# A third seven-product tile in the second matrix of a feed-forward layer, with one sum fewer per tile and later side work

## The chip, the cores and the metric

The kernel runs on one core of a Trainium2 chip. The metric is device time in microseconds of one launch. TensorE (PE) multiplies matrices into eight PSUM banks of 128 x 512 f32; VectorE (DVE) and ScalarE (ACT) do the elementwise work; SyncE (SP) issues the loads of weights.

## The reference

The reference is an encoder trunk of two layers over 256 tokens of width 2048. The change touches the feed-forward part of both layers:

```
def sq_relu_mlp(h, w1, w2):
    return jnp.square(jax.nn.relu(h @ w1)) @ w2

for i in range(DEPTH):                       # 2
    ... x = x + attention(rms_norm(x, ...))
    x = x + sq_relu_mlp(rms_norm(x, g), w1, w2)
return rms_norm(x, final_norm)
```

x is (1, 256, 2048) in float32, w1 is 2048 x 8192 and w2 is 8192 x 2048.

## The kernel before

Each float32 matrix is split into a high part that TensorE takes as it is (`wh`, by a cast on ACT) and the rest (`wl`, by a subtract on DVE); a product of two such matrices is three matmuls (`three`, L193).

A feed-forward layer (`ffn`) runs in four groups g. A group makes 2048 of the 8192 inner columns with two calls of `gemm_pair` on w1 (cp 0 and 1, 1024 columns each) and multiplies them by their rows of w2 with two more calls. A call is eight steps, called tiles here and counted from 1; tile n reads one weight block of 128 x 4 x 512 (two k-blocks by two column blocks), and its left matrix is pair k (two k-blocks of 128) of the normalized x, or of the inner activations `hT`. The tokens are two blocks, so a tile is a product of 2 x 2 block matrices.

A plain tile (kind "s") does the eight block products, 24 matmuls, into four banks named "2", "3", "4", "S". A tile of kind "x" does seven products in Strassen's manner (Winograd's form), 21 matmuls, of which some go to four more banks, "1", "5", "6", "7". It takes sums of weight blocks, made by `prep_x`: `sums` on DVE, their high parts `hs` on ACT, their low parts `ls` on DVE. It also takes sums of the left blocks, made once by `sums_and_parts` (four small subtracts on DVE, two casts on ACT, two subtracts on DVE). After the last x tile, `begin` combines banks "1", "6", "7", "5" into the tile `C`. `last_sum` (w1) or `early` and `put` (w2, into x) finish the sums. For w1 the result in `C` passes through relu and square on ACT (`squared_relu`), is transposed on TensorE in four groups of four, r = 0 to 3, each into a bank that the running call hasn't begun to use ("1", "6", "7", "5" in this order), and is read from there into `hT`.

FF_PAIRS = (3, 5) are the x tiles of all calls: tiles 4 and 6 of eight. The last call of a layer (g = 3, cp = 1) has another order of tiles, in which they are tiles 5 and 6 in the first layer and 3 and 5 in the second.

The order is written by hand. In step i, after each quarter's products, the program issues the side work that was attached to that quarter (`after`, `tasks`) and one part of the preparation of step i + 2:

```
        for n in range(4):
            s.quarters(s, n)
            ...
            elif i and n < 3:
                prep(i + 2, n)
        ...
        prep(i + 2, 3)
        load(i + 5)
```

Engines run their own queues in this order and wait for each other by semaphores. `w` has three buffers, `wh` and `wl` four each (two tiles' worth), `sums` one, `hs` and `ls` two.

Of the kernel before, what the change touches and what calls it, by code (L numbers as in the profile page):

```python
# [8 lines left out]
F32 = mybir.dt.float32  # L9
F32R = mybir.dt.float32r  # L10
# [4 lines left out]
P = 128  # L15
# [13 lines left out]
class Step:  # L29
# [6 lines left out]
    def __init__(self, kind, loads, quarters):  # L36
        self.kind = kind
        self.loads = loads
        self.quarters = quarters
        self.evac = []  # L40
        self.after = [[] for _ in range(4)]
        self.tasks = [[] for _ in range(4)]
        self.post = []
        self.hi, self.lo = [None] * 8, [None] * 8


@with_exitstack
def tile_encoder(ctx: ExitStack, tc: tile.TileContext, ins, out):
# [115 lines left out]
    def prep_x(s, n):  # L164

        w = s.w
        if n == 0:
            t = s.sums = part.pool.tile([P, 4, 512], F32, name="sums", tag="sums", bufs=1)
            add(nc.vector, t[:, 0:2, :], w[:, 1:3, :], w[:, 0, :].unsqueeze(1).to_broadcast([P, 2, 512]))
            add(nc.vector, t[:, 2, :], t[:, 1, :], w[:, 1, :])  # L170
            add(nc.vector, t[:, 3, :], t[:, 2, :], w[:, 3, :])
        elif n == 1:
            hi, lo = two_parts(s, 1)
            split(hi, lo, w[:, 2:4, :])
            s.hs = part.pool.tile([P, 4, 512], F32R, name="hs", tag="hs", bufs=2)
            nc.scalar.copy(s.hs, s.sums)  # L176
        elif n == 2:
            ls = part.pool.tile([P, 4, 512], F32R, name="ls", tag="ls", bufs=2)
            subtract(nc.vector, ls, s.sums, s.hs.bitcast(F32))
            for a in range(4):  # L180
                s.hi[4 + a], s.lo[4 + a] = s.hs[:, a, :], ls[:, a, :]
        else:
            hi, lo = two_parts(s, 0)
            split(hi[:, 1, :], lo[:, 1, :], w[:, 1, :])

    def block(w, k, c):
        return w[k, c // 512].rearrange("p (a n) -> p a n", n=512)
# [92 lines left out]
    def gemm_pair(w, cp, A, sums_of, order, finish, split_end=False):  # L280
        made, q = [], {}
        first_x = [n for n, o in enumerate(order) if o[0] == "x"]
        touched = set()

        def left(pair, which):

            t, u = A[pair // 2], 2 * (pair % 2)
            if which in ("S2", "S3", "S4"):
                c = sums_of[pair]
                return [c[:, h, ("S3", "S2", "S4").index(which), :] for h in range(2)]  # L290
            a, ts_ = {"A11": (0, 0), "A12": (1, 0), "S1": (0, 1), "A21": (0, 1), "A22": (1, 1)}[which]
            return [t[:, u + a, h, ts_ * P:(ts_ + 1) * P] for h in range(2)]

        def product(bank, a, b, last):
            if not q:
                q.update({k: banks[:, n, :] for k, n in sum_banks().items()})
            three(q[bank], a, b, bank not in touched, last)
            touched.add(bank)

        X = (("1", "A11", 2), ("2", "A12", 3), ("6", "S2", 6), ("7", "S3", 4), ("4", "A22", 7), ("3", "S4", 1),  # L300
             ("5", "S1", 5))

        for n, (kind, pair) in enumerate(order):
            k, u = pair // 2, pair % 2
            loads = [(w[k, 2 * cp + c].rearrange("p (a n) -> p a n", n=512)[:, 2 * u:2 * u + 2, :],
                      2 - 2 * c, 4 - 2 * c) for c in (1, 0)]
            if kind == "x":
                def quarter(s, m, pair=pair, n=n):
                    for bank, a, b in X[2 * m:2 * m + 2]:
                        product(bank, left(pair, a), (s.hi[b], s.lo[b]), n == first_x[-1] and bank in "1567")  # L310
            else:
                def quarter(s, m, pair=pair, n=n):
                    tb, c = QUARTERS[m]
                    for kk in range(2):
                        b = 2 * (1 - c) + kk
                        a = (("A11", "A12"), ("A21", "A22"))[tb][kk]
                        product(STD[tb, c], left(pair, a), (s.hi[b], s.lo[b]), n == len(order) - 1 and kk == 1)
            s = Step(kind, loads, quarter)
            s.even = pair % 2 == 0
            steps.append(s)  # L320
            made.append(s)

        if split_end:
            ends = made[-2:]
            for e, s in enumerate(ends):
                def quarter(s, m, e=e):
                    tb, m = m // 2, m % 2
                    pair = order[len(order) - 2 + m][1]
                    for kk in range(2):
                        b = 2 * (1 - e) + kk  # L330
                        a = (("A11", "A12"), ("A21", "A22"))[tb][kk]
                        product(STD[tb, e], left(pair, a), (ends[m].hi[b], ends[m].lo[b]), m == 1 and kk == 1)
                s.quarters = quarter

        def begin(m):
            if m == 0:
                C = q["C"] = part.pool.tile([P, 4, 512], F32, name="C", tag="C")
                nc.scalar.copy(C[:, 0, :], q["1"])
                subtract(nc.vector, C[:, 1, :], q["6"], C[:, 0, :])
            elif m == 1:  # L340
                subtract(nc.vector, q["C"][:, 2, :], q["C"][:, 1, :], q["7"])
            elif m == 2:
                add(nc.vector, q["C"][:, 1::2, :], q["C"][:, 1:3, :], q["5"].unsqueeze(1).to_broadcast([P, 2, 512]))

        s = made[first_x[-1] + 1]
        for m in range(3):
            s.after[0 if s is made[-1] else m].append(lambda m=m: begin(m))
        finish(made, q)
        return made
# [305 lines left out]
        return pending_norm(lambda: norms[n], n == 2)  # L655

    FF_PAIRS = (3, 5)
    FF_ORDER = [("x" if k in FF_PAIRS else "s", k) for k in range(8)]

    parts = {len(steps) + 9: "feed-forward"}  # L660
    out_rows(ins["na_wo"], na_oT, 4, lambda: norms[1], begin_norm(1, False, FF_PAIRS),
# [2 lines left out]

    def ffn(norm, w1, w2, next_norm, next_done):
        for g in range(4):
            hT, sums = [None] * 4, {}

            def hidden(made, q, cp, hT=hT, sums=sums):
                i = steps.index(made[-1]) + 1  # L670

                def squared_relu(tb, n):
# [7 lines left out]
                for r in range(4):  # L680
# [10 lines left out]
                    def post(r=r, held=held):  # L691
                        c, half, pair = 2 * cp + r // 2, r % 2, 4 * cp + r
                        if half == 0:
                            hT[c] = opool.tile([P, 4, 2, T], F32R, name="hT", tag="o")
                        if pair in FF_PAIRS:
                            raw = scratch([P, 2, T], "h")
                            nc.scalar.copy(raw, held["t"])
                            sums[pair] = part.pool.tile([P, 2, 3, P], F32R, name="hs", tag="hsum", bufs=len(FF_PAIRS))
                            sums_and_parts(raw, hT[c], half, sums[pair])
                        else:  # L700
                            to = hT[c][:, 2 * half:2 * half + 2]
                            split(to[:, :, 0, :], to[:, :, 1, :], held["t"])

                    at(i + 1 + r // 2, pe, post, quarter=r % 2 * 2)

            for cp in range(2):
                gemm_pair(w1, 2 * g + cp, norm.xT, norm.sums, FF_ORDER, lambda made, q, cp=cp: hidden(made, q, cp))

            w2g = w2[4 * g:4 * (g + 1)]
            last = g == 3  # L710

            def to(cp, tb, c):
                return x[:, tb, cp * 1024 + c * 512:cp * 1024 + (c + 1) * 512]

            def residual(made, q, cp, parted):
                def put(tb, c):
                    add(nc.vector, to(cp, tb, c), to(cp, tb, c), q[STD[tb, c]])

# [7 lines left out]
                        add(nc.vector, to(cp, 1, 1), to(cp, 1, 1), C[:, 3, :])  # L726

                if not parted:
                    for n in range(2):
                        made[-1].after[n].append(lambda n=n: early(n))  # L730
                    for m, (tb, c) in enumerate(QUARTERS):
                        made[-1].after[m].append(lambda tb=tb, c=c: put(tb, c))
                    if last:
                        for c in (2 * cp, 2 * cp + 1):
                            made[-1].post.append(lambda c=c: next_norm().squares(c))
                            if next_done is not None:
                                next_done(made[-1], c, c % 2)
                    return
# [15 lines left out]

            for cp in range(2):
                parted = last and cp == 1
                order = FF_ORDER
                if parted:
                    order = [FF_ORDER[k] for k in ((0, 1, 2, 4, 3, 5, 6, 7), (0, 1, 3, 2, 5, 4, 6, 7))[next_done is None]]
                gemm_pair(w2g, cp, hT, sums, order, lambda made, q, cp=cp, parted=parted: residual(made, q, cp, parted),  # L760
                          parted)

    ffn(norms[1], ins["ffn0_w1"], ins["ffn0_w2"], lambda: norms[2], begin_norm(2, True))
# [361 lines left out]
```

## Time and profile before

| | |
|---|---|
| median of 3 runs | 2296.74 us (2296.55 to 2297.01) |
| profiled execution | 2296.8 us, of it the span 2295.0 us |
| granted TensorE clock, mean | 0.998 |
| PE / PEld / DVE / ACT busy | 99% / 83% / 77% / 53% |
| DVE, all subtracts `wl<-w,wh` | 931.7 us, 802 of them |
| DVE, `ls<-sums,hs` | 146.7 us, 64 of them |
| DVE, waiting for `hs` ahead of `ls` | 44.4 us, 64 times |

The first number of a group in the profile is its busy time, then the mean of one in ns, then the idle time of that engine just before them with what ended it. A wait row reads: the engine and its line, what it waited for, us in total, times, the longest. A timeline row reads: start, duration, engine, line, operation, written from read.

### The profile page before, as it was taken

How to read it: one execution, taken by the hardware profiler on the slowest of the kernel's cores; microseconds unless marked ns; L12 is line 12 of the kernel's file. 1: busy time of each engine (PE TensorE's matmuls, PEld its weight loads, DVE VectorE, ACT ScalarE, POOL GpSimd, SP SyncE). 2: the span in 40 equal slices, each digit the busy share in tenths (PEclk: the TensorE clock that was granted, in tenths of full speed). 3: DMA queues.
4: the chain of work that ended last, by engine and by line, in shares of the span. 5: the costliest groups of instructions: out<-in, count | busy, mean ns of one | idle time of the engine just before them, and what ended most of it. 6: DMA issues, size and time to landing. Idle time of an engine off the chain costs nothing.

```text
span 2295.0 us, 28363 instructions
## 1 busy us (share of the span) xinstructions
PE 2269.6 (99%) x10988; PEld 1898.5 (83%) x10988; DVE 1758.1 (77%) x2065; ACT 1217.3 (53%) x1526; POOL 0.7 (0%) x6
## 2 busy tenths in 40 slices
PE   9999999999999999999999999999999999999998
PEld 7888888888888888888888888888888888888886
DVE  6666766788788788788877667757788788788787
ACT  6454545664565565465444544456654554554554
POOL 0000000000000000000000000000000000000000
PEclk9999999999999999999999999999999999999999
DMA  7566555656656656655555545545566566566563
GB/s 249 170 179 179 184 179 175 192 171 217 199 166 218 198 170 211 198 178 183 184 194 168 185 169 180 179 167 164 183 210 193 184 205 198 183 202 202 183 218 131
DMA packets 110727, 430.33 MB, mean 188 GB/s; under 512 B 23872, under 2 KB 24448, under 8 KB 92160
## 3 DMA queue, kind: packets, MB, share of 16 engines
q1 hardware_dynamic: 109920, 426.82, 57.7%
q8 instruction: 86, 1.41, 0.2%
q10 hardware_dynamic: 672, 1.70, 0.2%
q14 instruction: 49, 0.40, 0.0%
HBM read 426.38 MB, written 2.10 MB: 187 GB/s over the span
## 4 chain that ended last, share of the span: by engine, by line
PE 94%; DVE 3%; ACT 1%; DMA 1%; issue 1%; SPq 0%; ACTq 0%; DVEq 0%
PE banks L196 24%; PE banks L197 24%; PE banks L195 24%; PE banks L220 13%; PE banks L222 7%; PE banks L688 1%; DMA bias<-in_rpb_dram 1%; DVE wl L191 1%; PE banks L378 1%; ACT wh L190 1%; DVE x L136 0%; DVE sums L136 0%; PE banks L880 0%; PE banks L840 0%; PE banks L591 0%
## 5 line engine op out<-in xcount | busy, mean ns | idle before, releaser
L191 DVE TENSOR_TENSOR wl<-w,wh 128x1024 fp32r<-128x1024 f32 (+1 forms) x802 | 931.7, 1176 | 378.4 <-ACT wh L190 373.9
L190 ACT CAST wh<-w 128x1024 fp32r<-128x1024 f32 (+1 forms) x802 | 804.0, 1014 | 685.5 <-PE banks L197 447.7
L220 PE MATMUL banks<-xT,wh 128*128 128x512 f32 x1280 | 454.0, 398 | 0.9 <-ACT wh L190 0.7
L195 PE MATMUL banks<-wh,xT 128*128 128x512 f32 x1152 | 453.9, 394 | 0.0
L196 PE MATMUL banks<-wl,xT 128*128 128x512 f32 x1152 | 448.9, 390 | 0.9 <-DVE wl L191 0.9
L197 PE MATMUL banks<-wh,xT 128*128 128x512 f32 x1152 | 449.6, 390 | 0.0
L222 PE MATMUL banks<-xT,wl 128*128 128x256 f32 x1280 | 358.4, 280 | 2.3 <-DVE wl L191 2.3
L195 PE MATMUL banks<-wh,hT 128*128 128x512 f32 x832 | 327.7, 394 | 0.0
L197 PE MATMUL banks<-wh,hT 128*128 128x512 f32 x832 | 324.7, 390 | 0.0
L196 PE MATMUL banks<-wl,hT 128*128 128x512 f32 x832 | 323.9, 389 | 0.0
L220 PEld LDWEIGHTS banks<-xT,wh 128*128 128x128 f32 x1280 | 240.8, 188 | 55.6 <-ACT wh L190 1.8
L197 PEld LDWEIGHTS banks<-wh,xT 128*128 128x128 f32 x1152 | 216.3, 188 | 45.6
L196 PEld LDWEIGHTS banks<-wl,xT 128*128 128x128 f32 x1152 | 216.6, 188 | 44.8 <-DVE wl L191 1.9
L195 PEld LDWEIGHTS banks<-wh,xT 128*128 128x128 f32 x1152 | 216.5, 188 | 42.9
L222 PEld LDWEIGHTS banks<-xT,wl 128*128 128x128 f32 x1280 | 242.3, 189 | 3.4 <-DVE wl L191 3.2
L176 ACT CAST hs<-sums 128x2048 fp32r<-128x2048 f32 x64 | 122.5, 1914 | 153.2 <-DVE sums L136 153.2
L197 PEld LDWEIGHTS banks<-wh,hT 128*128 128x128 f32 x832 | 156.2, 188 | 33.2
L196 PEld LDWEIGHTS banks<-wl,hT 128*128 128x128 f32 x832 | 156.4, 188 | 31.6
L195 PEld LDWEIGHTS banks<-wh,hT 128*128 128x128 f32 x832 | 156.3, 188 | 31.3
L133 DVE TENSOR_TENSOR ls<-sums,hs 128x2048 fp32r<-128x2048 f32 x64 | 146.7, 2293 | 44.4 <-ACT hs L176 44.4
L136 DVE TENSOR_TENSOR sums<-sums,w 128x512 f32<-128x512 f32 x128 | 88.6, 692 | 4.4
L136 DVE TENSOR_TENSOR sums<-w 128x1024 f32<-128x1024 f32 x64 | 78.0, 1219 | 0.0
(187 smaller groups left out, 2142.0 us busy)
## 6 DMA issues: line engine op xcount, KB each, us to landing
w<-in_ffn_w_dram SPq DMA_DIRECT2D x512, 512.0 KB, 5.0
w<-in_dil_wqkv_dram SPq DMA_DIRECT2D x72, 1024.0 KB, 4.9
w<-in_na_wqkv_dram SPq DMA_DIRECT2D x47, 1024.0 KB, 5.1
w<-in_na_wo_dram SPq DMA_DIRECT2D x16, 1024.0 KB, 4.9
w<-in_dil_wo_dram SPq DMA_DIRECT2D x8, 1024.0 KB, 4.9
bias<-in_rpb_dram SPq DMA_DIRECT2D x32, 96.0 KB, 9.0
out_dram<-x SPq DMA_DIRECT2D x8, 256.0 KB, 2.5
x<-in_x_dram SPq DMA_DIRECT2D x3, 512.0 KB, 9.6
```

The costliest lines, as they stand in the source:

```text
L133: engine.tensor_tensor(out=out, in0=a, in1=b, op=ALU.subtract)
L136: engine.tensor_tensor(out=out, in0=a, in1=b, op=ALU.add)
L176: nc.scalar.copy(s.hs, s.sums)
L190: nc.scalar.copy(dst_hi, src)
L191: nc.vector.tensor_tensor(out=dst_lo, in0=src, in1=dst_hi.bitcast(F32), op=ALU.subtract)
L195: nc.tensor.matmul(o, left[0], right[0], start=start, stop=False)
L196: nc.tensor.matmul(o, left[0], right[1], start=False, stop=False)
L197: nc.tensor.matmul(o, left[1], right[0], start=False, stop=stop)
L220: nc.tensor.matmul(o, s.hi[a][:, cs], xt.rearrange("p h t -> p (h t)"), start=first, stop=False)
L222: nc.tensor.matmul(o[:, :T], s.lo[a][:, cs], xt[:, 0, :], start=False, stop=last)
L378: nc.tensor.transpose(self.tp[:, a, tb * P:(tb + 1) * P], x[:, tb, kt * P:(kt + 1) * P], ident)
L688: nc.tensor.transpose(t[:, a, tb * P:(tb + 1) * P], q["C"][:, 2 * tb + f // 4, f % 4 * P:(f % 4 + 1) * P], ident)
```

## The change

For the second matrix of groups 0 to 2 of both layers, pair 2 joins the x tiles. The order of pairs becomes 0, 1, 2, 4, 3, 6, 5, 7, so that x tiles are tiles 3, 5 and 7. The first matrix and the whole last group keep two.

The sum that A22 takes is added into the weight tile itself (`w[:, 0]`) and split there with `w[:, 1]`; `sums`, `hs` and `ls` are three blocks wide instead of four. This holds for all x tiles of the kernel.

The sums of the inner activations (`parts_of`) are moved from the tile of the transposes to later ones: pair 2 in tile 5, pair 3 in tile 6 of the second call, pair 5 in tile 4 of the third. The transposes of the second call's result, until now two groups in each of tiles 2 and 3 of the third call, are all in tile 2, in groups 0 to 2. `early`, the addition of C to x, moves from the last tile to tiles 3 and 5, or 4 and 6, of the next call. Since the last x tile is now tile 7, the three parts of `begin` all stand in tile 8.

```diff
@@ class Step
-        self.hi, self.lo = [None] * 8, [None] * 8
+        self.hi, self.lo = [None] * 7, [None] * 7
@@ prep_x
-            t = s.sums = part.pool.tile([P, 4, 512], F32, name="sums", tag="sums", bufs=1)
+            t = s.sums = part.pool.tile([P, 3, 512], F32, name="sums", tag="sums", bufs=1)
...
-            add(nc.vector, t[:, 3, :], t[:, 2, :], w[:, 3, :])
+            add(nc.vector, w[:, 0, :], t[:, 2, :], w[:, 3, :])
...
-            s.hs = part.pool.tile([P, 4, 512], F32R, name="hs", tag="hs", bufs=2)
+            s.hs = part.pool.tile([P, 3, 512], F32R, name="hs", tag="hs", bufs=2)
...
-            split(hi[:, 1, :], lo[:, 1, :], w[:, 1, :])
+            split(hi, lo, w[:, 0:2, :])
@@ gemm_pair
-        X = (... ("7", "S3", 4), ("4", "A22", 7), ("3", "S4", 1),
+        X = (... ("7", "S3", 4), ("4", "A22", 0), ("3", "S4", 1),
@@ ffn
+            last = g == 3
+            pairs2 = FF_PAIRS if last else (2, 3, 5)
@@ hidden
-                        if pair in FF_PAIRS:
-                            raw = scratch([P, 2, T], "h")
+                        if pair in pairs2:
+                            raw = part.pool.tile([P, 2, T], F32, name="h", tag="h", bufs=2)
                             nc.scalar.copy(raw, held["t"])
-                            sums[pair] = part.pool.tile([P, 2, 3, P], F32R, name="hs", tag="hsum", bufs=len(FF_PAIRS))
-                            sums_and_parts(raw, hT[c], half, sums[pair])
+
+                            def parts_of(c=c, half=half, raw=raw, pair=pair):
+                                sums[pair] = part.pool.tile([P, 2, 3, P], F32R, name="hs", tag="hsum", bufs=3)
+                                sums_and_parts(raw, hT[c], half, sums[pair])
+                            steps[i + (3 if cp else 2 + r)].after[1].append(parts_of)
...
-                    at(i + 1 + r // 2, pe, post, quarter=r % 2 * 2)
+                    if cp and not last:
+                        at(i + 1, pe, post, quarter=r)
+                    else:
+                        at(i + 1 + r // 2, pe, post, quarter=r % 2 * 2)
@@ residual
                 if not parted:
+                    i = steps.index(made[-1])
                     for n in range(2):
-                        made[-1].after[n].append(lambda n=n: early(n))
+                        if last:
+                            made[-1].after[n].append(lambda n=n: early(n))
+                        else:
+                            at_after(i + 1 + (2 + 2 * n if cp else 3 + 2 * n), 1, lambda n=n: early(n))
@@ second product
-                order = FF_ORDER
+                order = range(8) if last else (0, 1, 2, 4, 3, 6, 5, 7)
...
-                gemm_pair(w2g, cp, hT, sums, order, ...
+                gemm_pair(w2g, cp, hT, sums, ff_order(pairs2, order), ...
```

How it stands in the queues of ACT and DVE, at three places of a group. First ACT's queue at the start of the third call (w2, cp 0), tile 1 and the start of tile 2. The rows from C are relu and square of one quarter each; `hT<-banks` reads a transposed group, and `h<-banks` one whose sums are made. Before:

```order
L190 CAST wh<-w 128x1024 x4
L674 ACTIVATE C<-C,rstd 128x512
L675 ACTIVATE C<-C 128x512
L674 ACTIVATE C<-C,rstd 128x512
L675 ACTIVATE C<-C 128x512
L190 CAST wh<-w 128x1024
L674 ACTIVATE C<-C,rstd 128x512
L675 ACTIVATE C<-C 128x512
L674 ACTIVATE C<-C,rstd 128x512
L675 ACTIVATE C<-C 128x512
L190 CAST wh<-w 128x1024
L190 CAST hT<-banks 128x2x256
```

After (the lines of the file have moved by four):

```order
L190 CAST wh<-w 128x1024 x4
L678 ACTIVATE C<-C,rstd 128x512
L679 ACTIVATE C<-C 128x512
L678 ACTIVATE C<-C,rstd 128x512
L679 ACTIVATE C<-C 128x512
L190 CAST wh<-w 128x1024
L176 CAST hs<-sums 128x1536
L678 ACTIVATE C<-C,rstd 128x512
L679 ACTIVATE C<-C 128x512
L678 ACTIVATE C<-C,rstd 128x512
L679 ACTIVATE C<-C 128x512
L190 CAST wh<-w 128x1024
```

The cast `hs` of the first x tile, which is tile 3 now, has come between the second and the third pair of relu and square.

Second, DVE's queue for the x tile 6 of the second call (w1, cp 1), from the subtract of the tile ahead. Before, the sums of pair 3's activations stand ahead of that tile's `sums`:

```order
L133 TENSOR_TENSOR c<-h 128x128
L133 TENSOR_TENSOR c<-h,c 128x128
L133 TENSOR_TENSOR hT<-h,hT 128x2x256
L133 TENSOR_TENSOR hs<-c,hs 128x384
L191 TENSOR_TENSOR wl<-w,wh 128x1024
L136 TENSOR_TENSOR sums<-w 128x1024
L136 TENSOR_TENSOR sums<-sums,w 128x512 x2
L191 TENSOR_TENSOR wl<-w,wh 128x1024
L133 TENSOR_TENSOR ls<-sums,hs 128x2048
```

After:

```order
L191 TENSOR_TENSOR wl<-w,wh 128x1024 x3
L136 TENSOR_TENSOR sums<-w 128x1024
L136 TENSOR_TENSOR sums<-sums,w 128x512
L136 TENSOR_TENSOR w<-sums,w 128x512
L191 TENSOR_TENSOR wl<-w,wh 128x1024
L133 TENSOR_TENSOR ls<-sums,hs 128x1536
L191 TENSOR_TENSOR wl<-w,wh 128x1024
L133 TENSOR_TENSOR c<-h 128x128
```

The sums of the activations (`c<-h` and on) have gone behind the x tile's preparation, and the last of the weight sums is written into `w`.

Third, DVE's queue at the end of a w2 call, tile 8. Before:

```order
L136 TENSOR_TENSOR C<-C,banks 128x2x512
L191 TENSOR_TENSOR wl<-w,wh 128x1024
L136 TENSOR_TENSOR x<-x,C 128x1024
L136 TENSOR_TENSOR x<-x,banks 128x512
L133 TENSOR_TENSOR x<-x,C 128x512
L136 TENSOR_TENSOR x<-x,C 128x512
L136 TENSOR_TENSOR x<-x,banks 128x512
L191 TENSOR_TENSOR wl<-w,wh 128x1024
L136 TENSOR_TENSOR x<-x,banks 128x512 x2
```

After:

```order
L133 TENSOR_TENSOR C<-banks,C 128x512
L133 TENSOR_TENSOR C<-C,banks 128x512
L136 TENSOR_TENSOR C<-C,banks 128x2x512
L136 TENSOR_TENSOR x<-x,banks 128x512 x2
L191 TENSOR_TENSOR wl<-w,wh 128x1024
L136 TENSOR_TENSOR x<-x,banks 128x512 x2
L191 TENSOR_TENSOR wl<-w,wh 128x1024
```

The three operations on `C` now stand directly ahead of the additions of the banks to x, and the three additions of C to x are no longer there.

More of the change, by code (lines that the diff above doesn't have):

```diff
@@ L174, in prep_x @@
             split(hi, lo, w[:, 2:4, :])
-            s.hs = part.pool.tile([P, 4, 512], F32R, name="hs", tag="hs", bufs=2)
+            s.hs = part.pool.tile([P, 3, 512], F32R, name="hs", tag="hs", bufs=2)
             nc.scalar.copy(s.hs, s.sums)
         elif n == 2:
-            ls = part.pool.tile([P, 4, 512], F32R, name="ls", tag="ls", bufs=2)
+            ls = part.pool.tile([P, 3, 512], F32R, name="ls", tag="ls", bufs=2)
             subtract(nc.vector, ls, s.sums, s.hs.bitcast(F32))
-            for a in range(4):
+            for a in range(3):
                 s.hi[4 + a], s.lo[4 + a] = s.hs[:, a, :], ls[:, a, :]
@@ L298, in product @@
             touched.add(bank)
-        X = (("1", "A11", 2), ("2", "A12", 3), ("6", "S2", 6), ("7", "S3", 4), ("4", "A22", 7), ("3", "S4", 1),
+        X = (("1", "A11", 2), ("2", "A12", 3), ("6", "S2", 6), ("7", "S3", 4), ("4", "A22", 0), ("3", "S4", 1),
              ("5", "S1", 5))
@@ L657, in tile_encoder, with ff_order @@
     FF_PAIRS = (3, 5)
-    FF_ORDER = [("x" if k in FF_PAIRS else "s", k) for k in range(8)]
+    def ff_order(pairs, order=range(8)):
+        return [("x" if k in pairs else "s", k) for k in order]
     parts = {len(steps) + 9: "feed-forward"}
@@ L666, in ffn, with hidden @@
         for g in range(4):
+            last = g == 3
+            pairs2 = FF_PAIRS if last else (2, 3, 5)
             hT, sums = [None] * 4, {}
-            def hidden(made, q, cp, hT=hT, sums=sums):
+            def hidden(made, q, cp, hT=hT, sums=sums, pairs2=pairs2, last=last):
                 i = steps.index(made[-1]) + 1
@@ L702, in post, with residual @@
                             split(to[:, :, 0, :], to[:, :, 1, :], held["t"])
-                    at(i + 1 + r // 2, pe, post, quarter=r % 2 * 2)
+                    if cp and not last:
+                        at(i + 1, pe, post, quarter=r)
+                    else:
+                        at(i + 1 + r // 2, pe, post, quarter=r % 2 * 2)
             for cp in range(2):
-                gemm_pair(w1, 2 * g + cp, norm.xT, norm.sums, FF_ORDER, lambda made, q, cp=cp: hidden(made, q, cp))
+                gemm_pair(w1, 2 * g + cp, norm.xT, norm.sums, ff_order(FF_PAIRS), lambda made, q, cp=cp: hidden(made, q, cp))
             w2g = w2[4 * g:4 * (g + 1)]
-            last = g == 3
             def to(cp, tb, c):
                 return x[:, tb, cp * 1024 + c * 512:cp * 1024 + (c + 1) * 512]
-            def residual(made, q, cp, parted):
+            def residual(made, q, cp, parted, last=last):
                 def put(tb, c):
@@ L756, in ffn @@
                 parted = last and cp == 1
-                order = FF_ORDER
+                order = range(8) if last else (0, 1, 2, 4, 3, 6, 5, 7)
                 if parted:
-                    order = [FF_ORDER[k] for k in ((0, 1, 2, 4, 3, 5, 6, 7), (0, 1, 3, 2, 5, 4, 6, 7))[next_done is None]]
-                gemm_pair(w2g, cp, hT, sums, order, lambda made, q, cp=cp, parted=parted: residual(made, q, cp, parted),
+                    order = ((0, 1, 2, 4, 3, 5, 6, 7), (0, 1, 3, 2, 5, 4, 6, 7))[next_done is None]
+                gemm_pair(w2g, cp, hT, sums, ff_order(pairs2, order), lambda made, q, cp=cp, parted=parted: residual(made, q, cp, parted),
                           parted)
```

## The prediction

> **What bounds the kernel now.** A "tile" is one step of eight in a call of `gemm_pair`; a "plain" tile does eight block products, an "x tile" seven. I read the page first, then the chain of waits, then the stretches tile by tile, then TensorE's own waits.
>
> ```profile
> span 2295.0 us, 28363 instructions
> PE 2269.6 (99%) x10988; PEld 1898.5 (83%) x10988; DVE 1758.1 (77%) x2065; ACT 1217.3 (53%) x1526; POOL 0.7 (0%) x6
> PE 94%; DVE 3%; ACT 1%; DMA 1%; issue 1%; SPq 0%; ACTq 0%; DVEq 0%
> ```
>
> TensorE (PE) is busy all the time and carries 94% of the chain. DVE at 77% is an average; what counts is whether it keeps ahead in the tiles that change. One second-product call with its neighbours, by call (from and to; length; busy time and instructions of PE, PEld, DVE, ACT, POOL; granted clock, DMA share, GB/s):
>
> ```profile
> 580.93:623.27 42.34, 42.34 (x187) 34.92 (x186) 34.41 (x35) 20.09 (x19) 0.00 (x0) 1.00 0.64 197
> 623.27:667.77 44.50, 44.50 (x204) 36.42 (x203) 36.30 (x41) 27.39 (x33) 0.00 (x0) 1.00 0.59 189
> 667.77:712.05 44.28, 44.28 (x204) 36.48 (x203) 36.48 (x41) 27.40 (x33) 0.00 (x0) 1.00 0.59 190
> 712.05:754.39 42.34, 42.34 (x187) 34.92 (x186) 34.59 (x35) 20.10 (x19) 0.00 (x0) 1.00 0.63 198
> ```
>
> These are the four calls of one group: two of the first matrix, two of the second. The third, by tile (tiles 1, 2, 4, 6, 8):
>
> ```profile
> 667.77:673.21 5.44, 5.44 (x26) 4.50 (x25) 2.86 (x4) 5.15 (x8) 0.00 (x0) 1.00 0.64 194
> 673.21:679.58 6.37, 6.37 (x34) 5.29 (x33) 4.03 (x5) 4.32 (x6) 0.00 (x0) 1.00 0.44 134
> 685.95:690.82 4.87, 4.87 (x23) 3.95 (x21) 4.78 (x8) 4.26 (x6) 0.00 (x0) 1.00 0.46 135
> 696.31:701.17 4.86, 4.86 (x23) 3.93 (x22) 4.86 (x5) 3.04 (x4) 0.00 (x0) 1.00 0.35 78
> 706.61:712.05 5.44, 5.44 (x26) 4.50 (x25) 5.01 (x6) 2.11 (x2) 0.00 (x0) 1.00 0.72 239
> ```
>
> A plain tile takes 5.44 us for 24 matmuls (0.227 each), an x tile 4.86 for 21 (0.231 each), at a granted clock of 1.00. Tile 2 with two groups of four transposes takes 0.93 more, so 0.465 a group. The only waits of TensorE inside the feed-forward calls are these:
>
> ```profile
> PEld banks L196 <- DVE ls L133: 5.9, 10, 1.6
> PE banks L196 <- DVE ls L133: 2.1, 2, 1.2
> ```
>
> They are for `ls`, the low parts of the sums of an x tile. One of the eight small ones, then the two large ones (in the last calls, where x tiles stand elsewhere):
>
> ```profile
> 653.12 0.39 PE L195 MATMUL banks<-hs,xs 128*128 128x512 f32 x1
> 653.46 0.50 PE L196 MATMUL banks<-ls,xs 128*128 128x512 f32 x1
> 653.80 0.40 PE L197 MATMUL banks<-hs,xs 128*128 128x512 f32 x1
> ...
> 1088.81 0.39 PE L195 MATMUL banks<-hs 128*128 128x512 f32 x1
> 1090.36 0.51 PE L196 MATMUL banks<-ls,hs 128*128 128x512 f32 x1 [1.16 <-DVE ls L133]
> ...
> 2253.23 0.39 PE L195 MATMUL banks<-hs 128*128 128x512 f32 x1
> 2254.57 0.50 PE L196 MATMUL banks<-ls,hs 128*128 128x512 f32 x1 [0.95 <-DVE ls L133]
> ```
>
> From start to start 0.23 is normal. The first costs 0.68 - 0.46 = 0.22, the others 1.55 - 0.23 = 1.3 and 1.34 - 0.23 = 1.1.
>
> **The change, part by part.**
>
> *Twelve tiles become x tiles* (three groups, two calls, two layers). Each drops 3 matmuls. By the rows that is 5.44 - 4.86 = 0.58; the other end is 3 x 0.227 = 0.68, if a new x tile kept a plain tile's pace. I take 0.58, since all x tiles shown run at it: 12 x 0.58 = **-7.0 us** (end: -8.2). [...]
>
> *The sums shrink from four to three.* What an x tile's preparation costs now:
>
> ```profile
> 646.45 1.22 DVE L136 TENSOR_TENSOR sums<-w 128x1024 f32<-128x1024 f32 x1
> 647.71 1.42 DVE L136 TENSOR_TENSOR sums<-sums,w 128x512 f32<-128x512 f32 x2
> 649.05 1.22 DVE L191 TENSOR_TENSOR wl<-w,wh 128x1024 fp32r<-128x1024 f32 x1
> 651.11 2.29 DVE L133 TENSOR_TENSOR ls<-sums,hs 128x2048 fp32r<-128x2048 f32 x1 [0.84 <-ACT hs L176]
> ...
> L191 DVE TENSOR_TENSOR wl<-w,wh 128x512 fp32r<-128x512 f32 x68 | 46.3, 684 | 0.0
> L190 ACT CAST wh<-w 128x1024 fp32r<-128x1024 f32 x734 | 764.2, 1051 | 685.5 <-PE banks L197 447.7 <-PE banks L220 174.4 <-DVE x L136 23.3
> L176 ACT CAST hs<-sums 128x2048 fp32r<-128x2048 f32 x64 | 122.5, 1914 | 153.2 <-DVE sums L136 153.2
> ```
>
> From first sum to the end of `ls` is 6.95 us, and DVE stands 0.84 of it waiting for `hs`. After, between the 1024 and 2048 wide rows, `hs` of 1536 takes 1.48 and `ls` 1.76 (estimates), and the copy can start 0.7 earlier, since it no longer awaits the last 512-wide sum (1.42 for two). DVE then doesn't stand: 2.6 + 1.2 + 1.76, about 5.5 us, so `ls` is there **1.4 earlier**. Given back is a split of 1024 for 512 (1.22 for 0.68) behind `ls`; its half is first used by A22 in the third quarter, 1.4 us after `ls` is, and is ready 1.1 after it. The DVE work of a preparation stays 6.8 (1.22 + 1.42 + 1.22 + 1.76 + 1.22). So the two large waits (1.3, 1.1) go: **-2.4**. The eight small ones go too: their tile is prepared 1.4 earlier, and the 2.5 us of sums of activations that stood ahead of it moves behind it:
>
> ```profile
> 642.51 0.29 DVE L133 TENSOR_TENSOR c<-h 128x128 f32<-128x128 f32 x1
> ...
> 644.48 0.55 DVE L133 TENSOR_TENSOR hs<-c,hs 128x384 fp32r<-128x384 f32 x1
> ```
>
> (642.51 to 645.03.) That is 8 x 0.22 = **-1.8**. If something else is late there: 0.
>
> *DVE's added work*, costed at nothing, with DVE's own idle time as cover. A plain preparation is 2 x 1.22 = 2.4, an x one 6.8: +4.4 for each second-product call, which makes 36.5 + 4.4 = 40.9 in the third call (its end is then near 43.7) and 34.6 + 4.4 = 39.0 in the fourth (of 41.8), before the additions to x that leave the third for the fourth. In steady alternation DVE has 6.8 + 2.4 = 9.2 for each 5.44 + 4.86 = 10.3 of TensorE; once a group the sums of pair 5 make it 11.7, and 1.4 of backlog are worked off in the next two pairs. Preparation runs up to two tiles ahead, so a lag of that size is covered. In the second call it is 36.3 + 2.5 - 0.7 = 38.1 of 44.3. If the cover is gone, `ls` is late again, at 0.2 to 1.3 a tile, the range of the rows above.
>
> *Four transposes in tile 2 of the third call*, no longer two each in tiles 2 and 3: the same 4 x 0.465 on TensorE, no gain or loss. But the first x tile comes one tile sooner, and its first product writes the bank from which the first transposes are read. What stands before that read on ACT:
>
> ```profile
> 667.97 1.05 ACT L190 CAST wh<-w 128x1024 fp32r<-128x1024 f32 x1 [1.67 <-PE banks L197]
> 668.92 0.72 ACT L674 ACTIVATE C<-C,rstd 128x512 f32<-128x512 f32 x1
> ...
> 670.96 0.63 ACT L675 ACTIVATE C<-C 128x512 f32<-128x512 f32 x1
> 671.49 1.03 ACT L190 CAST wh<-w 128x1024 fp32r<-128x1024 f32 x1
> ```
>
> Counted from the call's start at 667.77: the second cast ends at +4.75; then, newly, `hs` (1.5, to +6.2), two more pairs of relu and square (2.6, to +8.8), a cast (1.0), DVE's subtract behind it (1.2, to +11.0) and the read of the bank (0.7, to +11.7). The x tile begins at 5.44 + 5.44 + 4 x 0.465 = +12.7. That leaves 1.0, or about 0.4 if DVE comes 0.6 late with the sums, since the second call's later parts push it. Cost 0; each us beyond it costs 6 us in all (six groups). The third and fourth transposes need the squares by +10.4 and have them at +8.8.
>
> *Later additions to x; sums of C all in the last tile.* Seven DVE operations there, none over 1.22 (the widest, 128x1024), behind about 2.4 of subtracts: the three that free banks end by 2.4 + 3.7 = 6.1 after the tile's start, and the next call's first tile reaches the last of these banks at 5.44 + 3 x 1.36 = 9.5; the four plain banks are wanted 16 after and free by 11. The additions from C stand in tiles where DVE has room. SP's queue keeps its order; a load waits for the last split of the tile three before it, two preparations (9 us) ahead of its use.
>
> The sum: -7.0 - 2.4 - 1.8 = -11.2. The profiled execution took 2296.8 (span 2295.0, 1.8 around it), against a median of 2296.74: **2285.6 us**.
>
> **Rivals.** 0.2% (4.6 us) is what a measurement here can tell from no change.
>
> 1. *The early x tile waits for its bank.* For it: ACT's chain is serial, and the slack is 0.4 to 1.0. Against it: it needs a further delay. At 0.7 late in each of six groups: 2285.6 + 4.2 = 2289.8.
> 2. *No change.* `ls` stays late by the small 0.22 in each of the 24 x tiles 5 and 7 (5.3 us), and the 4.2 of old waits isn't won: 2296.8 - 7.0 + 5.3 = 2295.1. For it: DVE's 94% of the third call. Against: the 0.84 that DVE no longer stands.
> 3. *Slower: DVE becomes the bound of the second product.* If an x and a plain preparation together need over 10.3 us, every second x tile starts late and never recovers. At the 1.1 of the last call for each of those 24 tiles: 2296.8 - 7.0 + 26.4 = 2316. It decides from 9.2 upwards by 1.1 a pair. Against it: DVE's rows follow each other without gaps (646.45 + 1.22 to 647.71; the next starts before the recorded end). [...]
>
> **How the numbers follow.** The sum above 0.72, rival 1 0.14, rival 2 0.08, rival 3 0.06. The first's own range is 2284 (twelve tiles at 0.68) to 2288 (half the old waits stay). With rival 1 and some more, 2284.0 to 2291.5 holds a little over 8 in 10. Faster by over 0.2%: 0.72 + 0.14 = 0.86; within: 0.08; slower: 0.06.
>
> **What would show it.** Third and fourth calls near 43.7 and 41.8 us; no TensorE wait for `ls`; `hs` near 1.5; no DVE wait for `hs` near 0.84. Wrong, if TensorE's waits name the subtract of `hT` (rival 1), or `ls` or `wl` in tiles 5 and 7 (rivals 2 and 3).

## The result, and the profile after

The changed kernel takes 2284.24 us (median, 2282.74 to 2285.37) against 2296.64 for the one before: a ratio of 0.9946, 95% interval 0.9929 to 0.9964, or 12.4 us less. Timed again beside the last experiment it gave 2284.24 against 2296.18 (0.9948, 0.9936 to 0.9961). The forecast was 2285.6.

The page of the profile after:

```profile
span 2280.9 us, 28400 instructions
PE 2258.6 (99%) x10952; PEld 1892.0 (83%) x10952; DVE 1810.2 (79%) x2143; ACT 1242.4 (54%) x1550; POOL 0.7 (0%) x6
PE 96%; DVE 1%; DMA 1%; ACT 1%; issue 0%; SPq 0%; ACTq 0%; DVEq 0%
```

TensorE's matmuls fell by 36, its share of the chain rose from 94% to 96%, and DVE's busy time rose by 52 us without making any call longer. The four calls of the same group, the second of four in the first layer (columns as in the prediction):

```profile
577.74:620.09 42.35, 42.35 (x187) 34.92 (x186) 36.05 (x37) 20.12 (x19) 0.00 (x0) 1.00 0.64 196
620.09:664.30 44.21, 44.21 (x203) 36.48 (x202) 37.11 (x45) 28.64 (x35) 0.00 (x0) 1.00 0.59 187
664.30:707.92 43.62, 43.62 (x200) 35.91 (x199) 39.03 (x44) 28.67 (x34) 0.00 (x0) 1.00 0.65 203
707.92:749.68 41.76, 41.76 (x184) 34.35 (x183) 38.43 (x39) 21.50 (x20) 0.00 (x0) 1.00 0.64 200
```

Against before: first call the same, second -0.29, third -0.66, fourth -0.58. The third call by tile (tiles 2 to 7):

```profile
669.74:676.93 7.19, 7.19 (x41) 5.98 (x40) 5.48 (x6) 6.55 (x10) 0.00 (x0) 1.00 0.33 111
676.93:681.89 4.96, 4.96 (x24) 4.03 (x23) 4.35 (x6) 2.48 (x3) 0.00 (x0) 1.00 0.71 214
681.89:687.34 5.45, 5.45 (x26) 4.50 (x24) 5.37 (x7) 2.63 (x3) 0.00 (x0) 1.00 0.48 170
687.34:692.18 4.84, 4.84 (x22) 3.94 (x21) 4.43 (x7) 3.77 (x5) 0.00 (x0) 1.00 0.74 220
692.18:697.63 5.45, 5.45 (x25) 4.50 (x24) 5.38 (x6) 3.38 (x3) 0.00 (x0) 1.00 0.63 193
697.63:702.48 4.85, 4.85 (x23) 3.94 (x21) 3.91 (x4) 2.61 (x3) 0.00 (x0) 1.00 0.61 193
```

The three x tiles (3, 5 and 7) take 4.85 each, and tile 3 some 0.1 more behind the fourth group of transposes: its second matmul starts 0.32 after its first instead of 0.23. DVE is busy for 5.37 of 5.45 in tile 4 and 5.38 in tile 6, and has its rest in the x tiles (4.43 of 4.84 in tile 5, 3.91 of 4.85 in tile 7). No TensorE wait for `ls` is left. The two operations of the sums, each in all:

```profile
L133 DVE TENSOR_TENSOR ls<-sums,hs 128x1536 fp32r<-128x1536 f32 x76 | 133.1, 1751 | 0.3 <-ACT hs L176 0.3
L176 ACT CAST hs<-sums 128x1536 fp32r<-128x1536 f32 x76 | 112.9, 1485 | 119.5 <-DVE sums L136 119.5
```

DVE stood 44.4 us waiting for `hs` before, and 0.3 now, with twelve more of them.

### The profile page after: what moved, and what is told of

Read it like the earlier page. It is cut to its first block, busy times and chain, and to the rows that moved or that the text cites. A ratio compares the mean times of both kernels' runs of the same rounds, so it can differ in the third digit from the quotient of the medians.

```text
span 2280.9 us, 28400 instructions
## 1 busy us (share of the span) xinstructions
PE 2258.6 (99%) x10952; PEld 1892.0 (83%) x10952; DVE 1810.2 (79%) x2143; ACT 1242.4 (54%) x1550; POOL 0.7 (0%) x6
## 4 chain that ended last, share of the span: by engine, by line
PE 96%; DVE 1%; DMA 1%; ACT 1%; issue 0%; SPq 0%; ACTq 0%; DVEq 0%
PE banks L195 25%; PE banks L197 25%; PE banks L196 24%; PE banks L220 13%; PE banks L222 7%; PE banks L692 1%; DMA bias<-in_rpb_dram 1%; PE banks L378 1%; DVE wl L191 1%; ACT wh L190 0%; PE banks L893 0%; PE banks L853 0%; PE banks L591 0%; DMA x<-in_x_dram 0%; DVE x L136 0%
## 5 line engine op out<-in xcount | busy, mean ns | idle before, releaser
L191 DVE TENSOR_TENSOR wl<-w,wh 128x1024 fp32r<-128x1024 f32 (+1 forms) x802 | 967.9, 1218 | 355.3 <-ACT wh L190 352.1
L190 ACT CAST wh<-w 128x1024 fp32r<-128x1024 f32 (+1 forms) x802 | 832.5, 1048 | 653.7 <-PE banks L197 389.4
L195 PE MATMUL banks<-wh,xT 128*128 128x512 f32 x1184 | 466.2, 394 | 0.0
L197 PE MATMUL banks<-wh,xT 128*128 128x512 f32 x1184 | 461.8, 390 | 0.0
L196 PE MATMUL banks<-wl,xT 128*128 128x512 f32 x1184 | 460.8, 389 | 0.5 <-DVE wl L191 0.5
L195 PE MATMUL banks<-wh,hT 128*128 128x512 f32 x804 | 316.6, 394 | 0.0
L197 PE MATMUL banks<-wh,hT 128*128 128x512 f32 x804 | 313.7, 390 | 0.0
L197 PEld LDWEIGHTS banks<-wh,xT 128*128 128x128 f32 x1184 | 222.2, 188 | 47.2
L195 PEld LDWEIGHTS banks<-wh,xT 128*128 128x128 f32 x1184 | 222.5, 188 | 44.2
L176 ACT CAST hs<-sums 128x1536 fp32r<-128x1536 f32 x76 | 112.9, 1485 | 119.5 <-DVE sums L136 119.5
L133 DVE TENSOR_TENSOR ls<-sums,hs 128x1536 fp32r<-128x1536 f32 x76 | 133.1, 1751 | 0.3 <-ACT hs L176 0.3
L136 DVE TENSOR_TENSOR sums<-w 128x1024 f32<-128x1024 f32 x76 | 92.6, 1218 | 0.0
L195 PE MATMUL banks<-wh,oT 128*128 128x512 f32 x192 | 76.5, 398 | 0.0
```

The source lines that it names most:

```text
L133: engine.tensor_tensor(out=out, in0=a, in1=b, op=ALU.subtract)
L136: engine.tensor_tensor(out=out, in0=a, in1=b, op=ALU.add)
L190: nc.scalar.copy(dst_hi, src)
L191: nc.vector.tensor_tensor(out=dst_lo, in0=src, in1=dst_hi.bitcast(F32), op=ALU.subtract)
L195: nc.tensor.matmul(o, left[0], right[0], start=start, stop=False)
L196: nc.tensor.matmul(o, left[0], right[1], start=False, stop=False)
```

## The experiments

In the tables of calls below, lengths are from the first matmul of a call to that of the next. Sums over both layers add up such lengths for all calls. E2, E3 and E5 were timed once each, so their argument rests on the calls of their traces more than on the time.

**E1, the smaller sums alone.** The kernel before, with three sums in `prep_x` and A22 taken from `w`, and nothing else:

```diff
-            add(nc.vector, t[:, 3, :], t[:, 2, :], w[:, 3, :])
+            add(nc.vector, w[:, 0, :], t[:, 2, :], w[:, 3, :])
...
-            split(hi[:, 1, :], lo[:, 1, :], w[:, 1, :])
+            split(hi, lo, w[:, 0:2, :])
```

> The kernel before with the smaller sums alone: sums, hs and ls three blocks wide, the last sum written into w; no more x tiles and no side work moved. Theory (ls comes 1.4 us earlier, and that is enough): all ten waits for ls go, the last calls of the layers get 1.5 and 1.25 shorter, the second calls go from 44.45 to 44.21 each, in all -4.6, about 2292.0. Rival (the small waits went because the sums of activations were moved behind the x tile): the second calls stay at 44.45, only the two last calls gain, about 2293.9.

Measured: 2291.48 against 2295.77, ratio 0.9982 (0.9972 to 0.9991), 4.3 us less. Its four calls:

```profile
581.35:623.70 42.35, 42.35 (x187) 34.94 (x186) 34.32 (x35) 20.10 (x19) 0.00 (x0) 1.00 0.63 197
623.70:667.91 44.21, 44.21 (x203) 36.50 (x202) 36.11 (x41) 27.71 (x33) 0.00 (x0) 1.00 0.59 192
667.91:712.18 44.27, 44.27 (x203) 36.47 (x202) 36.32 (x41) 27.49 (x33) 0.00 (x0) 1.00 0.58 189
712.18:754.53 42.35, 42.35 (x188) 34.93 (x186) 34.51 (x35) 20.09 (x19) 0.00 (x0) 1.00 0.62 199
```

The second call is at 44.21 already, so the small waits go with the smaller sums, and the moved sums of activations aren't needed for that. By the starts of the calls the two layers gain 2.7 and 2.1, in all 4.8. From here to the changed kernel it is 3.65 + 3.7 = 7.3, nearly all of it the twelve x tiles.

**E2, the old copy `hs`.** The changed kernel, with four sums and `hs` of four blocks again (the fourth block's low part is a separate subtract in the place where its split stood):

```diff
-            add(nc.vector, w[:, 0, :], t[:, 2, :], w[:, 3, :])
+            add(nc.vector, t[:, 3, :], t[:, 2, :], w[:, 3, :])
...
-            s.hs = part.pool.tile([P, 3, 512], F32R, name="hs", tag="hs", bufs=2)
+            s.hs = part.pool.tile([P, 4, 512], F32R, name="hs", tag="hs", bufs=2)
```

> The changed kernel with the old form of hs: the copy is 2048 wide and waits for all sums, so that DVE stands about 0.8 us ahead of each ls again; ls itself stays 1536 wide. Theory (DVE's room in the third call comes from not standing there): ls of tile 7 of the third call has 2.0 us to spare in the changed kernel and loses 0.9 a tile, about 2.8 by the third x tile, so the third calls get 0.5 to 1 longer than 43.62, first of all by a wait for ls in tile 7; in all +3 to +6 on the changed kernel, some 2287 to 2290. Rival (DVE has room anyway, 79% busy): no TensorE wait for ls, third calls 43.6, time as the changed kernel, 2284.

Measured: 2290.01 in one run, 5.8 above the changed kernel. Third and fourth call, tile 2 of the third, how DVE stands before `ls`, and the wait for squares:

```profile
666.08:710.12 44.04, 43.99 (x201) 35.79 (x199) 39.85 (x47) 28.46 (x34) 0.00 (x0) 1.00 0.60 190
710.12:752.00 41.88, 41.88 (x185) 34.37 (x183) 39.01 (x43) 21.27 (x20) 0.00 (x0) 1.00 0.65 213
...
671.52:678.98 7.46, 7.41 (x42) 5.91 (x40) 5.77 (x7) 6.70 (x9) 0.00 (x0) 1.00 0.36 120
...
L133 DVE TENSOR_TENSOR ls<-sums,hs 128x1536 fp32r<-128x1536 f32 x76 | 133.7, 1759 | 57.5 <-ACT hs L176 57.5
...
PEld banks L694 <- ACT C L681: 2.9, 6, 0.5
```

The time came as my theory said, but not from the place. The third call is 0.42 longer, yet only 0.07 of it is in tile 7, where I looked for it. Most is in tile 2 (7.46 against 7.19), where the third transposes wait for squares on ACT, because `hs` stands ahead of them and ends later. The two last calls give 1.0 and 0.8 (`ls` again), and nearly every plain tile behind an x tile took 5.47 to 5.49 instead of 5.45, some 2.7 us over the kernel. In the tile that begins at 600.52, for instance, the first ten matmuls take until 602.84, 2.32 instead of 2.27; no wait is recorded among them, and why they are slower stays open. The x tiles still pay in this form: third and fourth calls are 44.04 and 41.88 against 44.27 and 42.35 in E1.

**E3, sums of activations at once.**

```diff
-                            steps[i + (3 if cp else 2 + r)].after[1].append(parts_of)
+                            parts_of()
```

> The changed kernel with the sums of the inner activations made at once after the transposes, as before, and not in later tiles. Theory (the move is needed): in the third call the 2.5 us of pair 5 stand ahead of the read of the bank of the third transposes, so TensorE waits about 1.1 in tile 3 for a read of hT; in the second call 5 us less 1.1 of idle time stand ahead of ls of tile 6, which has 3.8 to spare, a wait of 0.2 at most. Six groups: +7 to +8, about 2292. Rival (the move only tidies): third calls 43.6, time as the changed kernel, 2284.

Measured: 2293.82 in one run, 9.6 above the changed kernel. Second and third call, and TensorE's waits (those for `hT` are in the third calls, those for `ls` and six of those for `wl` in the second):

```profile
623.07:667.89 44.82, 44.77 (x204) 36.34 (x203) 37.77 (x46) 28.40 (x35) 0.00 (x0) 1.00 0.60 188
667.89:712.55 44.66, 43.89 (x201) 35.85 (x200) 38.79 (x43) 28.88 (x34) 0.00 (x0) 1.00 0.61 194
...
PE banks L195 <- DVE hT L191: 4.6, 6, 0.8
...
PEld banks L195 <- DVE hT L191: 7.2, 6, 1.2
...
PEld banks L196 <- DVE wl L191: 4.2, 8, 0.9
PEld banks L196 <- DVE ls L133: 2.7, 6, 0.5
```

The third call loses 1.04, to a read of `hT` in tile 3, six times in all; I had said 1.1. The second loses 0.6 in tile 6, where I had said at most 0.2: its weight loads wait up to 0.46 for `wl` and 0.45 for `ls`, six times each. So this move is needed, first of all for the bank.

**E4, additions to x back in the last tile.**

```diff
-                        if last:
+                        if True:
                             made[-1].after[n].append(lambda n=n: early(n))
```

> The changed kernel with the additions of C to x in the last tile of each call again, not in later tiles. Theory (DVE has 3.2 us to spare for ls of the first x tile of the fourth call and the additions take 2.6): no TensorE wait, all calls as in the changed kernel within 0.1, time the same, 2284. Rival (the move was needed): the 2.6 us push the first x tile of the fourth call, which then waits for ls, up to 1 us in each of three groups of two layers, +3 to +6, 2287 to 2290.

Measured: 2283.14 against 2295.77, ratio 0.9944 (0.9928 to 0.9961). Third and fourth call:

```profile
665.54:709.16 43.62, 43.62 (x201) 35.91 (x199) 39.01 (x43) 28.69 (x34) 0.00 (x0) 1.00 0.63 203
709.16:750.92 41.76, 41.76 (x185) 34.35 (x183) 38.42 (x39) 21.07 (x20) 0.00 (x0) 1.00 0.64 202
```

The calls are the same to a hundredth of a microsecond, and DVE's time in them to two. This part of the change, the moved additions, does nothing for the time.

**E5, transposes in tiles 2 and 3 again.**

```diff
-                    if cp and not last:
+                    if False:
                         at(i + 1, pe, post, quarter=r)
```

> The changed kernel with the transposes of the second call's result in tiles 2 and 3 of the third call again, two groups each, though tile 3 is an x tile now. Theory (the bank that an x tile writes must have been read; this is rival 1 of the prediction driven to its end): the third group's bank is wanted a quarter after its transposes and the fourth group's at once, each read stands behind some 3 to 5 us of DVE's work on the next x tile, so TensorE waits for reads of hT twice a group, 6 to 9 us in each of six groups: +36 to +54, about 2320 to 2338, all of it in the third calls. Rival (the reads are quick, 1.2 us each, DVE being ahead): +2.4 a group, about 2299.

Measured: 2324.61 in one run, 40 above. The third calls grew from 43.62 to between 48.6 and 52.2. The waits, and tiles 2 to 5 of one of these calls (8th number: granted clock):

```profile
PE banks L195 <- DVE hT L191: 27.0, 12, 3.1
...
676.64:683.01 6.37, 6.37 (x34) 5.29 (x33) 4.66 (x5) 6.05 (x9) 0.00 (x0) 1.00 0.27 104
683.01:696.67 13.66, 9.16 (x30) 6.75 (x29) 9.91 (x11) 5.59 (x6) 0.00 (x0) 0.68 0.49 154
696.67:702.82 6.15, 6.15 (x25) 5.00 (x24) 3.45 (x7) 2.17 (x3) 0.00 (x0) 0.88 0.52 171
702.82:707.67 4.85, 4.85 (x22) 3.94 (x21) 3.45 (x4) 2.50 (x3) 0.00 (x0) 1.00 0.26 59
```

There are two waits a group for reads of `hT`, the mechanism of the prediction's first rival, at 5.0 to 8.6 a call; I had said 6 to 9. Without the new place of the transposes the change would have cost 28 us instead of saving 12.

**E6, three x tiles in the first call too.** The changed kernel, where the w1 calls with cp 0 also take pairs 2, 3 and 5. The second call takes pair 2 plainly from parts that hold A21 - A22 instead of A21 here, so that the output differs.

```diff
+    W1_PAIRS = (2, 3, 5)
+    THREE = (0, 1, 2, 4, 3, 6, 5, 7)
...
-                gemm_pair(w1, 2 * g + cp, norm.xT, norm.sums, ff_order(FF_PAIRS), ...
+                gemm_pair(w1, 2 * g + cp, norm.xT, norm.sums, ff_order(FF_PAIRS) if cp else ff_order(W1_PAIRS, THREE), ...
```

> A step beyond the changed kernel: the first call of each group (w1, cp 0) also has x tiles 3, 5 and 7, with the sums of pair 2 of the normalized x. Theory (each x tile is worth 0.58 as long as DVE, 36.05 of 42.35 us busy there, has room for 4.0 more): the first calls go from 42.35 to 41.77, no new waits, 8 x 0.58 = -4.7 on the changed kernel, about 2279.5. Rival (tile 8 then holds three operations on C, four last sums and two preparations, and the squares of the next call come late): waits of 0.5 to 1 in each second call, -4.7 + 4 to 8, 2284 to 2288.

Measured: 2281.94 against 2296.69, ratio 0.9939 (0.9924 to 0.9955). First and second call, and the wait that came in ahead of the first layer:

```profile
580.75:622.51 41.76, 41.76 (x184) 34.36 (x183) 38.43 (x39) 21.49 (x20) 0.00 (x0) 1.00 0.61 202
622.51:666.72 44.21, 44.21 (x203) 36.48 (x202) 38.57 (x47) 28.63 (x35) 0.00 (x0) 1.00 0.57 180
...
PE banks L378 <- DVE x L475: 2.1, 2, 1.8
```

The calls do what the theory said, 8 x 0.59, and the second isn't touched. But the norm's sums of pair 2 delay the additions to x in the attention's last steps, and TensorE waits 1.8 there before it can transpose (0.3 in the changed kernel). The first layer begins at 408.47 here, and at 408.51 and 408.97 in the two later runs with this order, where the other profiles have 404.88 to 407.30. The gain that is left over the changed kernel is 2.3 by the medians, and the intervals of the two ratios overlap.

**E7, in both first-matrix calls.** The order of E6 for cp 0 and cp 1, and all transposes of the first call's result in tile 2 of the second.

```diff
-                gemm_pair(w1, 2 * g + cp, norm.xT, norm.sums, ff_order(FF_PAIRS), ...
+                gemm_pair(w1, 2 * g + cp, norm.xT, norm.sums, ff_order(W1_PAIRS, THREE), ...
...
-                    if cp and not last:
+                    if not (cp and last):
```

> Both calls on w1 have three x tiles, and the transposes of the first call's result are all in tile 2 of the second. Theory (room in DVE: 37.1 of 44.21 us busy in the second call, 4.0 more makes 41.1 of 43.6): 16 x 0.58 = -9.3 on the changed kernel, 2275, or up to 2278 if the sums of pairs 2 and 3, which still stand in tiles 5 and 6 there, push ls of tile 7 by 0.4. Rival (the second call is the fullest now, with the sums of two pairs beside three x tiles, 94% of DVE): waits of 1 to 2 us in each second call, 2283 to 2291, no better than the changed kernel.

Measured: 2293.24 against 2296.69, ratio 0.9985 (0.9976 to 0.9994), so 9 us above the changed kernel. Second and third call, then TensorE's waits, then the second call of the last group:

```profile
624.54:669.30 44.76, 44.18 (x201) 35.77 (x199) 40.25 (x48) 29.70 (x36) 0.00 (x0) 1.00 0.55 172
669.30:714.39 45.09, 44.12 (x201) 35.87 (x200) 41.55 (x47) 28.79 (x34) 0.00 (x0) 1.00 0.62 202
...
PE banks L196 <- DVE wl L191: 4.2, 8, 0.6
PE banks L694 <- ACT C L681: 4.0, 6, 0.7
...
971.27:1015.09 43.82, 43.82 (x201) 35.85 (x200) 40.00 (x45) 28.87 (x34) 0.00 (x0) 1.00 0.60 191
```

My theory fell, and the time is above the rival's 2291 too. The second calls are 1.1 longer than the 43.6 it gave, as the rival said (most of it in tile 8, which takes 6.37 instead of 5.45 and waits there for `wl`), and the third, of which neither spoke, 1.5 longer than 43.62: what is late at the end of one call is paid in the next, where the transposes wait for squares and for their banks. The run holds a comparison of its own: in the last group the sums of pair 2's activations aren't made, and there tile 8 takes 5.45, the second call 43.82 (43.88 in the other layer) and the third 44.21, as in the changed kernel. So most of the loss comes with the second pair's sums, as the rival had it. DVE is busy for 90% of a second call that waits in tile 8 (40.25 of 44.76) and for 91% of the one that doesn't (40.00 of 43.82). That average shows nothing; what DVE still has to do at the call's end does.

**E8, E6 with S1 of pair 2 in a place of its own**, so that the second call has its A21 again. E9 is the changed kernel once more, in the same runs.

```diff
-        subtract(nc.vector, a21, a21, a22)
-        subtract(nc.vector, c[:, 1, :], a11, a21)
+        s1 = c[:, 3, :] if keep else a21
+        subtract(nc.vector, s1, a21, a22)
+        subtract(nc.vector, c[:, 1, :], a11, s1)
...
+            if which == "S1" and sums_of[pair].shape[2] == 4:
+                return [sums_of[pair][:, h, 3, :] for h in range(2)]
```

> The first call of each group with three x tiles as in the experiment before last, but the difference S1 of pair 2 of the normalized x has a place of its own, so that the second call can take pair 2 plainly. Theory (no feed-forward call is touched by it; only the norm's sums are 128 columns wider): first calls 41.76, others as in the changed kernel, and the wait of about 1.8 us for the additions to x ahead of the first layer's last transposes stays: 4.7 - 2 to 2.4 below the changed kernel, about 2281.9. Rival (the wider sums delay the norm's chain further): the wait ahead of the first layer grows beyond 3 us and nothing is left of the gain, 2284.

> The changed kernel itself once more, beside the one with three x tiles in the first calls, on the same chip and in more rounds. Both theories: 2284.2, 12.2 to 12.6 below the kernel before, every call as in its first profile within 0.05 us, with only the start of the program different between executions.

Measured: E8 2282.36 (2281.05 to 2282.84), E9 2284.24 (2283.36 to 2285.66), before 2296.18: ratios 0.9938 (0.9924 to 0.9951) and 0.9948 (0.9936 to 0.9961). E9's calls are those of the first profile within 0.02. E8's first calls are 41.77, the wait ahead of the first layer is 1.8 as in E6, and the time is near the 2281.9 of the theory. By the medians E8 is 1.9 us faster than the changed kernel. The two intervals against the kernel before overlap, but in these runs E8's highest time lies under E9's lowest.

## Why the prediction was right, point by point

| term | predicted | measured, both layers | shown by |
|---|---|---|---|
| twelve x tiles | -7.0 | -7.3 (third calls -3.7, fourth -3.5) | E1 to the changed kernel |
| two large waits for `ls` | -2.4 | -2.7 (last calls up to their tile 8: 40.25 and 38.16 to 38.76 and 36.91) | E1 |
| eight small waits | -1.8 | -1.9 (second calls) | E1 |
| plain tiles of the third calls | not in the sum | -0.3 | E1, and the last groups' third calls (44.28 and 44.26 to 44.21) |
| DVE's added work | 0 | 0 (39.03 of 43.62 and 38.43 of 41.76 busy; 40.9 and 39.0 were expected) | no wait for `ls` |
| transposes in tile 2 | 0 | 0 | E5 for the opposite |
| additions to x, sums of C | 0 | 0 | E4 for the additions; no wait for the sums of C |
| sum | -11.2 | -12.2 | |

The median moved by 12.4. The profiled execution moved by 14.1, of which 1.7 lie ahead of the feed-forward layers: its first layer begins at 404.88 us instead of 406.59, where E9, the same kernel, has 407.10. So the 1.7 is the spread of the program's start and no work of the change.

The terms were a little small. An x tile takes 4.85 as said, but tile 5 of the third call, a plain one, took 5.49 before:

```profile
690.82:696.31 5.49, 5.49 (x26) 4.51 (x25) 4.58 (x5) 2.87 (x3) 0.00 (x0) 1.00 0.84 265
```

The plain tiles behind x tiles take 5.45 now, and no wait is named there in either profile; I had costed named waits alone. And I read the size of the two large waits from one gap each, while the matmul behind it is 0.11 late too. My list of TensorE's waits inside the layers also left out two, of 1.2 and 0.3 us, in tile 8 of the first layer's last call, where the next norm's transposes wait for x; they are the same after the change.

The durations worked out between two rows held: `hs` 1.485 for 1.48, `ls` 1.751 for 1.76. So did the chain to the bank. ACT and DVE after, tile 3 beginning at 676.93:

```profile
672.92 1.03 ACT L190 CAST wh<-w 128x1024 fp32r<-128x1024 f32 x1
...
675.12 0.68 DVE L191 TENSOR_TENSOR hT<-banks,hT 128x512 fp32r<-128x512 f32 x1
```

The bank is read by 675.80, +11.5 after the call's start against +11.7 in the prediction, and 1.1 ahead of its use, where I had 0.4 to 1.0. For `ls` of tile 7 there are 2.2 to spare:

```profile
695.25 1.75 DVE L133 TENSOR_TENSOR ls<-sums,hs 128x1536 fp32r<-128x1536 f32 x1
...
699.23 0.40 PE L196 MATMUL banks<-ls,hs 128*128 128x512 f32 x1
```

It ends at 697.00, and its first matmul starts at 699.23.

One step gave the right result by a wrong reason. I laid the end of the small waits to two causes, the earlier `ls` and the sums of activations that move behind it. E1 shows that the first alone does all of it. E3 shows what the move is for: without it the new tile 3 of the third call waits for its bank and the second call's tile 6 for `wl` and `ls`, 9.6 us in all.

Rival 2 (no change) and rival 3 (DVE bound) failed: no wait for `ls` is left in tiles 5 and 7. The reason that I gave against rival 2, DVE no longer standing before `ls`, counts for less than I thought. E2 brings the standing back and loses nearly half the gain, but in the tiles that rival 2 names it loses only 0.07, in tile 7 of the third calls. Against rival 3 the sum of DVE's work held: a plain and an x preparation together stay under the time that TensorE takes for the two (in the third call DVE is busy for 9.80 of the 10.29 of tiles 4 and 5, and for 9.29 of the 10.30 of tiles 6 and 7). Rival 1 is real, as E3 and E5 show, but had 1.1 us to go.

## What to carry to other kernels

When a product is cut down and the engine that feeds it gets more to do, count its work per pair of tiles, and then look at what stands in its queue ahead of each read that frees a bank: here 40 us hung on where two groups of four transposes stand in each of six calls, and none on where the additions to x stand. An engine's stand-still (DVE before `ls`) is room for the next change, even where it costs little today: the smaller sums were worth 4.3 us by themselves, and with the old copy back the whole change gives up 5.8 of its 12.4. Average busy time hides the limit: DVE at 89% of the third call and 92% of the fourth cost nothing, while E7, with 90% in its second calls, lost 9 us, because of what was left to do at the call's end.

## What was not expected of the hardware

The third calls of E5, with waits of up to 3.1 us on TensorE, lost more than their waits. Matmuls of E5 from the wait of 3.10 in the second group's third call on, and then tile 3 of the first group's third call (8th number: granted clock):

```profile
688.76 0.80 PE L195 MATMUL banks<-hs 128*128 128x512 f32 x1 [3.10 <-DVE hT L191]
...
689.78 0.63 PE L197 MATMUL banks<-hs 128*128 128x512 f32 x1
690.21 0.63 PE L195 MATMUL banks<-wh,hT 128*128 128x512 f32 x1
...
506.05:516.80 10.75, 6.25 (x30) 4.68 (x29) 9.27 (x10) 5.58 (x6) 0.00 (x0) 1.00 0.63 195
```

In the second group the matmuls follow each other by 0.43 instead of 0.23. The granted clock of this tile 3 was 0.68 and of tile 4 0.88, and tile 4, a plain one, took 6.15 instead of 5.45. In four other groups tile 3 had 0.74 or 0.86. In the first group the same two waits, 3.10 and 1.40, left the clock at 1.00. Of the 6.7 us that a third call grew on average, 4.5 (27.0 in six) are recorded waits; the first group's, at a clock of 1.00, grew by 5.0, so some 1.7 of the 2.2 that remain go with the clock (an estimate from these calls). A lower clock came with these waits in five of six groups; what sets it off, and why the first group was spared, no run here shows.
